# A one-layer streaming encoder on one core: the right-hand side of SBUF moved by 64 bytes, the first gate's row fetched behind the first convolution block, and the stored blocks of W_out split during z's first four tiles

## The chip, the core and the metric

The kernel runs on one NeuronCore of a Trainium2 chip. The core has five engines, each with its own instruction queue in program order: PE (TensorE, matrix products into PSUM), DVE (VectorE), ACT (ScalarE), POOL (GpSimd) and SP (SyncE, which here only issues DMAs). They wait for one another through semaphores. SBUF holds 128 partitions; a tile's address below is its byte offset in each partition. A matmul has a stationary operand, which is loaded into the array first (the rows PEld of the profile), and a moving one, which streams through it column by column; both come from SBUF. The metric is the device time of one execution in microseconds (us), the median of several runs.

## The reference

One layer for 1024 tokens of width 1024, all in float32. `c` gives six modulation vectors; `gate_m` scales the mixer's result and `gate_f` that of the feed-forward part.

```python
c_act = jax.nn.silu(c)
mod = (c_act @ w_ada[l] + b_ada[l])[:, None, :]
sh_m, sc_m, g_m, sh_f, sc_f, g_f = jnp.split(mod, 6, axis=-1)
h = rmsnorm(x, norm_mix_w[l]) * (1 + sc_m) + sh_m
z, xbc, dt_raw, q, k, v = jnp.split(h @ w_in[l], IN_SPLITS, axis=-1)
y_ssd = ssd_mixer(z, xbc, dt_raw, ssd_conv_w[l], ssd_conv_b[l], dt_bias[l], a_log[l],
                  d_skip[l], ssd_norm_w[l])
y_att = chunk_attention(q, k, v, rel_bias[l])
x = x + g_m * (jnp.concatenate([y_ssd, y_att], axis=-1) @ w_out[l])
h = rmsnorm(x, norm_ffn_w[l]) * (1 + sc_f) + sh_f
x = x + g_f * conv_ffn(h, w_up[l], ffn_conv_w[l], w_down[l])
return rmsnorm(x, final_norm_w)
```

`ssd_mixer` convolves `xbc` (eight blocks of 128 channels) causally over time, runs a state-space scan in chunks, and multiplies by `silu(z)`; `conv_ffn` is an up product, a short convolution, a gated silu and a down product.

## The kernel before

**Precision.** Every large product is made of three matmuls of fp32r operands: `mm3` (lines 84 to 86) multiplies high by high, high by low and low by high part. `split` (lines 88 to 94) makes the two parts: ACT copies the high one, DVE subtracts to get the low one; with a scale they are lines 90 and 91.

**Stages, in order of time.** The modulation and the first projections (0 to 97 us); attention with the other projections; the convolution blocks of `xbc` (`conv_silu`: 24 x 2 matmuls of 512 columns each, then the taps of line 651 on DVE and silu on ACT); z (`z_tile`: eight tiles for each of two column halves, 24 matmuls of 260 columns a tile); the scan with the product by W_out (`ssd_pre`, `ssd_y`, `wout_half`); the up stage (22 `Unit`s, each seven products of 12 matmuls of 512 columns into `uX`, `uY` and `uZ`); the down stage (seven products into `dn`). Up and down use a scheme of seven half-size products.

**Where operands lie.** SBUF is filled from both ends. The left pools hold constants, the ring homes `w0`, `w1` (pool `rw`) and `w2` (`wu`), the high and low parts of h (`hH`, `hL`, later `tH`, `tL`); the right ones hold `pad`, `ya`, the attention tiles, `xs`, z's weights `wzh` and `wzl`, and later `b11`, `b21`, `t1` and the ring homes `r12` and `r22` (`hq`). In the built program the left tiles lie 64 bytes past a multiple of 128 (w0 at 3520, w1 at 11712, w2 at 19904, hH0 at 36288), the right ones at a multiple (r12 at 106368, r22 at 114560, t1h at 122752, b11h at 163712, ya at 212864); matmuls start at such addresses plus multiples of 128. `pad` (line 180) is never read or written: its size sets where the right side starts.

**The ring.** Split weights of the up stage, and both split operands of the down stage, take their homes in turn, so that the home of each `w` is known from its place in the order:

```python
HOMES = ((rw, "w0"), (rw, "w1"), (wu, "w2"), (hq, "r12"), (hq, "r22"))
FIRST, AGAIN = (0, 1, 2, 0, 1, 3, 4), (2, 0, 1, 3, 4)
```

In the down stage each step splits first the moving operand, then the stationary one.

**The first gate and W_out.** `mod_col` loads a row block of `w_ada` and reduces it on DVE; `conv_mods` spreads these over the convolutions. The columns of `gate_m` are added up in `gcol` (line 911), turned into rows by a matmul and an ACT copy, written to DRAM (`cols_to_dram`, lines 149 to 152) and read back as a row for all partitions (line 924) into `rowb` and `gm1`. W_out comes in eight slots of 128 x 1024. `wout_load` fetches a slot in two DMAs, `wout_fold` (line 737) multiplies a slot of the first column half by the gate's row, `wout_store` splits slots 4 to 7 and writes high and low parts to DRAM, `wout_split` splits slots 0 to 3 into h's place once z no longer reads it, `wout_back` fetches the stored ones. Slots 0 and 1 are staged in `wst`, the others in three thirds of `wos`: 4 and 7 share the first, 5 and 2 the second, 6 and 3 the third, so the later load of each pair waits for the earlier slot's store. Slots 4 to 7 are split at tiles 3 to 6 of z's second half (column half 1, which is computed first).

**z's weights.** `wz_weights` loads a half in four pieces through the two halves of `raws`, so that pieces 3 and 4 load only when pieces 1 and 2 are split.

**What sets the order.** A scheduler with a timing model orders each engine's instructions at build time, so a step may stand elsewhere than its line suggests.

Of the kernel before, what the change touches and what calls it, by code (L numbers as in the profile page):

```python
# [72 lines left out]
def tile_block(ctx: ExitStack, tc: tile.TileContext, x, ccol, pk, w_ada, w_first, w_ft, w_z,  # L73
               w_out, w_up, w_down, bias, fnw, out, dbg=None):
    nc = tc.nc
    V, A, T = (InOrder(tc, e) for e in (nc.vector, nc.scalar, nc.tensor))
# [20 lines left out]
    const = ctx.enter_context(tc.tile_pool(name="const", bufs=1))  # L97
# [12 lines left out]
    modc = const.tile([P, 48], F32, name="modc")  # L110
# [28 lines left out]
    def raw_tile(n=1024):  # L139
        rawc[0] += 1  # L140
        return raws[:, rawc[0] % 2, 0:n]

    def mod_col(ft, t, at=None):
        nc.sync.dma_start(t, w_ada[ft])
        with tc.issue_after(at) if at else ExitStack():
            V.tensor_tensor_reduce(out=t, in0=t, in1=rowa, scale=1.0, scalar=0.0,
                                   op0=ALU.mult, op1=ALU.add, accum_out=modc[:, ft:ft + 1])

    def cols_to_dram(cols, ps, t, d):
        T.matmul(ps, cols, ident, start=True, stop=True)  # L150
        A.activation(t, ps, AF.Copy)
        nc.sync.dma_start(d, t)
# [3 lines left out]
    def wu_pair(src, hieng, loeng):  # L156
        t = raw_tile()
        nc.sync.dma_start(t, src)
        wh = wu.tile([P, 1024], F32R, tag="wh", name="wh")
        if not wls:  # L160
            wls.append(wu.tile([P, 2, 1024], F32R, tag="w2", bufs=1, name="wl"))
        wl = wls[0][:, rawc[0] % 2, :]
        split(wh, wl, t, hieng, loeng)
        return wh, wl
# [12 lines left out]
        return ap.rearrange("p (a b) -> p a b", a=4)  # L177

    pad = ctx.enter_context(tc.tile_pool(name="pad", bufs=1, side="right"))
    pad.tile([P, 24], F32, name="pad")  # L180
    es_y = ExitStack()
    yp = es_y.enter_context(tc.tile_pool(name="yp", bufs=1, side="right"))
    es_at = ExitStack()
# [82 lines left out]
    def s_tile():  # L266
        return ps1.tile([P, 1024], F32, tag="s", bufs=2, name="s")
# [93 lines left out]
    for j in range(2):  # L361
        k = slice(4 * j, 4 * j + 4)
# [43 lines left out]
    for hh in range(2):  # L406
# [13 lines left out]
        for kt in range(KT):  # L420
            if hh == 0:
# [7 lines left out]
                t = raw_tile(768)  # L429
# [73 lines left out]
    def tp_tile():  # L503
        return pst.tile([P, 512], F32, tag="tp", bufs=2, name="tp")
# [139 lines left out]
    def conv_silu(ft, dst):  # L644
        wh, wl = early.pop(ft) if ft in early else wu_pair(w_ft[ft], A, V)
        ps = s_tile()
        gemm_ft(wh, wl, [ps[:, 0:512], ps[:, 512:1024]])
        w = [pkt[:, SCW + 4 * ft + j:SCW + 4 * ft + j + 1] for j in range(4)]
        A.activation(dst, ps, AF.Identity, scale=w[3], bias=pkt[:, SCB + ft:SCB + ft + 1])
        for j in range(1, 4):  # L650
            last = V.scalar_tensor_tensor(dst[:, j:S], ps[:, 0:S - j], w[3 - j], dst[:, j:S],
                                          op0=ALU.mult, op1=ALU.add)
        for hh in range(2):
            c = slice(hh * 512, hh * 512 + 512)
            A.activation(dst[:, c], dst[:, c], AF.Silu)
        return last.ins
# [18 lines left out]
    def th512():  # L675
        return thp.tile([P, 512], F32, tag="th", bufs=2, name="th")
# [16 lines left out]
    gm1 = es_g.enter_context(tc.tile_pool(name="gmp", bufs=1, side="left")).tile([P, 512], F32, name="gm1")  # L693
# [5 lines left out]
    def conv_mods(n, at):  # L699
        for _ in range(CMODS[n]):  # L700
            k = wosc[0]
            wosc[0] += 1
            t = xs[:, 2 * (k % 4):2 * (k % 4) + 2, :].rearrange("p a b -> p (a b)") if n < 5 else wos[:, k % 3, :]
            mod_col(todo.pop(0), t, at)

    conv_mods(0, last_v[0])
    for g in range(2):
        conv_mods(2 * g + 1, conv_silu(4 + g, bt_[g]))
        conv_mods(2 * g + 2, conv_silu(6 + g, ct_[g]))
    G.memset(ones, 1.0)  # L710
    G.affine_select(out=tle, in_=ones, compare_op=ALU.is_ge, fill=0.0, base=0,
# [17 lines left out]
    def wout_load(slot):  # L729
        (dh, j), t = WORDER[slot], stage(slot)  # L730
        for b in range(2):
            nc.sync.dma_start(t[:, b * 512:(b + 1) * 512], w_out[order[2 * j + b], :, halves[dh]])
        return t

    def wout_fold(t):
        tv = t.rearrange("p (a b) -> p a b", a=2)
        V.tensor_tensor(tv, tv, rowb[:, 0:512].unsqueeze(1).to_broadcast([P, 2, 512]), ALU.mult)
# [14 lines left out]
    def wout_store(slot, t):  # L752
        h = bcp.tile([P, D], F32R, tag="rm", bufs=2, name="woh")
        for b in range(2):
            c = slice(512 * b, 512 * b + 512)
            k = SNW + order[2 * WORDER[slot][1] + b]
            split(h[:, c], t[:, c].bitcast(F32R), t[:, c], A, V, scale=pkt[:, k:k + 1])
        nc.sync.dma_start(wsd[slot - 4][0], f32(h))
        nc.sync.dma_start(wsd[slot - 4][1], t)
# [3 lines left out]
            nc.sync.dma_start(f32(t), d)  # L763

    wsd = [[dram.tile([P, D], F32, name=f"ws{n}{k}") for n in "hl"] for k in range(4)]
    gmd, gfd = (dram.tile([8, P], F32, name=n) for n in ("gmd", "gfd"))
    acd = dram.tile([64, P], F32, name="acd")

    def rows_from(d, k, n):
        return d[k:k + n].unsqueeze(0).to_broadcast([P, n, P])  # L770

    wzp = es_t.enter_context(tc.tile_pool(name="wzp", bufs=1, side="right", reuse_waits="tile"))

    def wz_weights(ch):
        ws = []
        for a in range(4):
            th_ = wzp.tile([P, 2, 288], F32R, tag="wzh", bufs=WZB, name="wzh")[:, :, 0:260]
            tl_ = wzp.tile([P, 2, 288], F32R, tag="wzl", bufs=WZB, name="wzl")[:, :, 0:260]
            t = raw_tile(520)
            nc.sync.dma_start(t, w_z[ch, :, a * 520:(a + 1) * 520])  # L780
            split(th_, tl_, t.rearrange("p (a b) -> p a b", a=2), A, V, scale=(0.5, None)[ch])
            ws.append((th_, tl_))
        return ws
# [83 lines left out]
    def ssd_pre(c, xp_, between=None):  # L867
# [38 lines left out]
        return xdt, xdd, cb, ms_  # L906

    wz = wz_weights(1)
    gcol = const.tile([P, 16], F32, name="gcol")
    gbias = [pkt[:, B_ADA + o:B_ADA + o + 8] for o in (G_M, G_F)]  # L910
    V.tensor_tensor(gcol[:, 0:8], modc[:, G_M:G_M + 8], gbias[0], ALU.add)
    WORDER = [(0, 0), (0, 1), (1, 0), (1, 1), (0, 2), (0, 3), (1, 2), (1, 3)]
    wt = {}

    def wout_get(*slots):
        for j in slots:
            wt[j] = wout_load(j)

    for st in range(NT):
        z_tile(1, st, wz)  # L920
        if st == 0:
            cols_to_dram(gcol[:, 0:8], tp_tile()[0:8, 0:P], th512()[0:8, 0:P], gmd)
            for t, k in ((rowb[:, 0:512], 0), (gm1, 4)):
                nc.sync.dma_start(t.rearrange("p (a b) -> p a b", a=4), rows_from(gmd, k, 4))
            wout_get(0, 1, 4, 5, 6)
        if st == 2:
            V.tensor_tensor(gcol[:, 8:16], modc[:, G_F:G_F + 8], gbias[1], ALU.add)
            cols_to_dram(gcol[:, 8:16], tp_tile()[0:8, 0:P], th512()[0:8, 0:P], gfd)
        if st in (3, 4, 5, 6):
            j = st + 1  # L930
            if j < 6:
                wout_fold(wt[j])
            wout_store(j, wt[j])
            if j == 4:
                wout_get(7)
        if st in (6, 7):
            wout_fold(wt[st - 6])
    wz = wz_weights(0)
    wout_get(2, 3)
    for st in range(NT):  # L940
# [170 lines left out]
    for c in range(NT):  # L1111
        if c == 1:
            ssd_turn(*turn)
        y, t = ssd_y(c, *pre)
# [10 lines left out]
        n, k = ((0, slice(0, 3)), (2, slice(0, 4)), (3, slice(0, 3)))[c] if c < 3 else (c + 1, slice(0, 3))  # L1125
# [622 lines left out]
```

## Time and profile before

| | us |
|---|---|
| median of 3 runs (1190.01 to 1191.69) | 1190.08 |
| the profiled execution | 1191.6 |
| its span | 1189.9 |
| PE busy | 1162.9 |
| DVE busy | 910.1 |
| ACT busy | 587.5 |
| POOL busy | 163.0 |
| convolutions | about 255 to 355 |
| z | 355.6 to 409 |
| scan and W_out | 409 to 540 |
| up stage | 540 to 968 |
| down stage | 968 to 1185 |

The span is what the profile covers; the execution's own time has 1.7 us around it. A row of the timeline gives start, duration, engine, line, operation, output and inputs (buffer numbers left out), shape and count; in brackets stands how long the engine had been idle before it and what it waited for. A matmul's duration is modelled and longer than the distance to the next one, since they are pipelined: the pace is read from the starts. For `dn<-w` both operands are tiles called `w`.

### The profile page before, as it was taken

To read this page: it belongs to the slowest core of one execution; us is meant where nothing else is said; L and a number is where in the kernel's file an instruction comes from. 1 tells how busy PE (TensorE), PEld (TensorE's weight loads), DVE (VectorE), ACT (ScalarE), POOL (GpSimd) and SP (SyncE) were. 2 spreads that over 40 slices of the span, in tenths; PEclk is the share of its full clock that TensorE was granted. 3 is DMA by queue.
4 is the path that set the end of the run, shared out by engine and by line. 5 is a ranking of instruction groups with operands and counts; after the bars stand their busy time and mean duration, and the time that the engine had idled before them with its cause. 6 is when DMAs were issued, how large, how long until landed. Compare 5 with 4: busy or idle time off the path is not lost.

```text
span 1189.9 us, 15790 instructions
## 1 busy us (share of the span) xinstructions
PE 1162.9 (98%) x5839; PEld 974.3 (82%) x5839; DVE 910.1 (76%) x1357; ACT 587.5 (49%) x971; POOL 163.0 (14%) x179
## 2 busy tenths in 40 slices
PE   8999999999999999999999999999999999999996
PEld 7778888788889888887788888888888888888885
DVE  7746565687775778559999988898888869666986
ACT  5636555664334666586443444334533444433454
POOL 1103343440000266200000000000000000000522
PEclk9999999999999999999999999999999999999999
DMA  9736334254455722241223322332233378633443
GB/s 350 259 85 163 94 119 117 56 178 134 141 202 203 297 98 80 72 141 36 98 107 133 116 79 92 113 131 79 83 106 115 116 277 298 238 122 119 158 135 148
DMA packets 63741, 169.15 MB, mean 142 GB/s; under 512 B 6880, under 2 KB 7344, under 8 KB 62256
## 3 DMA queue, kind: packets, MB, share of 16 engines
q1 hardware_dynamic: 56320, 143.11, 36.1%
q10 hardware_dynamic: 7344, 25.04, 5.4%
q8 instruction: 46, 0.75, 0.3%
q14 instruction: 31, 0.25, 0.1%
HBM read 125.87 MB, written 32.81 MB: 133 GB/s over the span
## 4 chain that ended last, share of the span: by engine, by line
PE 81%; DVE 11%; ACT 3%; issue 3%; DMA 1%; POOL 1%; POOLq 0%; DVEq 0%; ACTq 0%
PE wops L854 6%; PE dn L86 5%; PE dn L84 5%; PE dn L85 5%; PE uY L84 5%; PE uY L86 5%; PE uY L85 5%; PE uX L86 3%; PE uX L84 3%; PE uZ L85 3%; PE uZ L84 3%; PE uX L85 3%; PE uZ L86 3%; PE s L84 3%; PE s L86 3%
## 5 line engine op out<-in xcount | busy, mean ns | idle before, releaser
L85 PE MATMUL dn<-w 128*128 128x512 f32 x296 | 108.1, 391 | 0.0
L84 PE MATMUL dn<-w 128*128 128x512 f32 x296 | 108.1, 391 | 0.0
L86 PE MATMUL dn<-w 128*128 128x512 f32 x296 | 100.2, 391 | 0.2 <-DVE w L94 0.2
L84 PE MATMUL uY<-tH,w 128*128 128x512 f32 x248 | 97.2, 392 | 0.0
L85 PE MATMUL uY<-tL,w 128*128 128x512 f32 x248 | 97.0, 391 | 0.0
L86 PE MATMUL uY<-tH,w 128*128 128x512 f32 x248 | 96.9, 391 | 0.0
L1609 POOL TENSOR_TENSOR ya<-ya,xs 128x512 f32<-128x512 f32 x4 | 17.2, 4334 | 557.4 <-ACT xs L1605 557.4
L93 ACT ACTIVATE w<-ya 128x1024 fp32r<-128x1024 f32 (+1 forms) x41 | 39.2, 957 | 87.2 <-PE uY L86 84.2
L854 PE MATMUL wops<-hH,yhl 128*128 128x512 f32 x224 | 73.0, 398 | 1.0 <-DVE yhl L94 1.0
L86 PEld LDWEIGHTS dn<-w 128*128 128x128 f32 x296 | 55.4, 188 | 13.3 <-DVE w L94 1.1
L535 POOL TENSOR_SCALAR p<-p,st 128x640 f32<-128x640 f32 (+4 forms) x64 | 50.3, 794 | 115.9 <-DVE st L534 113.0
L84 PEld LDWEIGHTS dn<-w 128*128 128x128 f32 x296 | 55.5, 188 | 12.4
L85 PEld LDWEIGHTS dn<-w 128*128 128x128 f32 x296 | 55.5, 188 | 12.2
L93 ACT ACTIVATE w<-xs 128x1024 fp32r<-128x1024 f32 (+1 forms) x41 | 39.1, 954 | 38.6 <-PE uY L86 33.3
L529 DVE CUSTOM_DVE_ANT_0 p<-s,bias 128x640 f32<-128x640 f32 (+4 forms) x58 | 38.3, 674 | 23.1 <-PE tp L561 8.8
L86 PEld LDWEIGHTS uY<-tH,w 128*128 128x128 f32 x248 | 46.6, 188 | 10.5
L84 PEld LDWEIGHTS uY<-tH,w 128*128 128x128 f32 x248 | 46.6, 188 | 10.3
L85 PEld LDWEIGHTS uY<-tL,w 128*128 128x128 f32 x248 | 46.5, 188 | 10.2
L532 ACT ACTIVATE p<-p,st 128x640 f32<-128x640 f32 (+4 forms) x64 | 44.1, 692 | 18.0 <-DVE st L529 17.3
L94 DVE TENSOR_TENSOR pt<-tp,pt 128x512 fp32r<-128x512 f32 (+2 forms) x72 | 41.8, 595 | 13.1 <-ACT pt L93 12.8
L1283 DVE SCALAR_TENSOR_TENSOR a<-cv,pkt,a 128x1023 f32<-128x1023 f32 (+1 forms) x40 | 51.0, 1278 | 0.1
L84 PE MATMUL s<-hH,wh 128*128 128x512 f32 x128 | 50.5, 395 | 0.1
(503 smaller groups left out, 3402.0 us busy)
## 6 DMA issues: line engine op xcount, KB each, us to landing
gz<-a ACTq DMA_DIRECT2D x10, 1024.0 KB, 5.0
ya<-in_w_up_dram SPq DMA_DIRECT2D x11, 768.0 KB, 4.2
xs<-in_w_up_dram SPq DMA_DIRECT2D x11, 768.0 KB, 4.1
adat<-in_w_ada_dram SPq DMA_DIRECT2D x16, 512.0 KB, 5.8
xs<-in_w_ada_dram SPq DMA_DIRECT2D x16, 512.0 KB, 4.5
raws<-in_w_ft_dram SPq DMA_DIRECT2D x15, 512.0 KB, 3.9
qk<-qk SPq DMA_DIRECT2D x56, 128.0 KB, 2.3
gy<-a ACTq DMA_DIRECT2D x10, 512.0 KB, 2.6
```

Source lines behind the costliest of these rows:

```text
L84: T.matmul(ps, lh, rh, start=start, stop=False, skip_group_check=more)
L85: T.matmul(ps, lh, rl, start=False, stop=False, skip_group_check=more)
L86: T.matmul(ps, ll, rh, start=False, stop=stop, skip_group_check=more)
L93: i = A.activation(hi, src, AF.Copy) if ehi is A else ehi.tensor_copy(hi, src)
L94: return i, elo.tensor_tensor(lo, src, f32(hi), ALU.subtract)
L529: V.tensor_tensor_reduce(out=dst, in0=src, in1=bsl, scale=-1.0, scalar=3e38, op0=ALU.add, op1=ALU.min, accum_out=nm)
L532: A.activation(pv_, pv_, AF.Exp, scale=-1.0, bias=nm, accum_out=rs)
L535: last_g.append(G.tensor_scalar(pv_, pv_, rr, 1.0, op0=ALU.mult, op1=ALU.mult).ins)
L854: i = op(*a, **k)
L1283: V.scalar_tensor_tensor(a[:, j:S], c[:, 0:S - j], w[2 - j], a[:, j:S], op0=ALU.mult, op1=ALU.add)
L1609: G.tensor_tensor(src, src, fnr[:, halves[1]], ALU.mult)
```

## The change

- `pad` has 8 floats instead of 24, so every tile of the right side lies 64 bytes higher; the left side stays. All matmul operands then lie 64 bytes past a multiple of 128.
- The columns of `gate_m`, their way through DRAM and the two row loads stand after the first convolution block (`g == 0`) instead of before and in z's first tile.
- In z's first tile the W_out slots are asked for in the order 4, 5, 6, 0, 1 instead of 0, 1, 4, 5, 6.
- Slots 4 to 7 are folded (the first two) and stored at tiles 0 to 3 instead of 3 to 6, and slots 0 and 1 are folded at tiles 4 and 5 instead of 6 and 7.

```diff
-    pad.tile([P, 24], F32, name="pad")
+    pad.tile([P, 8], F32, name="pad")
...
+    gcol = const.tile([P, 16], F32, name="gcol")
+    gbias = [pkt[:, B_ADA + o:B_ADA + o + 8] for o in (G_M, G_F)]
     conv_mods(0, last_v[0])
     for g in range(2):
         conv_mods(2 * g + 1, conv_silu(4 + g, bt_[g]))
+        if g == 0:
+            V.tensor_tensor(gcol[:, 0:8], modc[:, G_M:G_M + 8], gbias[0], ALU.add)
+            cols_to_dram(gcol[:, 0:8], tp_tile()[0:8, 0:P], th512()[0:8, 0:P], gmd)
+            for t, k in ((rowb[:, 0:512], 0), (gm1, 4)):
+                nc.sync.dma_start(t.rearrange("p (a b) -> p a b", a=4), rows_from(gmd, k, 4))
         conv_mods(2 * g + 2, conv_silu(6 + g, ct_[g]))
...
     for st in range(NT):
         z_tile(1, st, wz)
         if st == 0:
-            cols_to_dram(gcol[:, 0:8], tp_tile()[0:8, 0:P], th512()[0:8, 0:P], gmd)
-            for t, k in ((rowb[:, 0:512], 0), (gm1, 4)):
-                nc.sync.dma_start(t.rearrange("p (a b) -> p a b", a=4), rows_from(gmd, k, 4))
-            wout_get(0, 1, 4, 5, 6)
+            wout_get(4, 5, 6, 0, 1)
...
-        if st in (3, 4, 5, 6):
-            j = st + 1
+        if st in (0, 1, 2, 3):
+            j = st + 4
             if j < 6:
                 wout_fold(wt[j])
             wout_store(j, wt[j])
             if j == 4:
                 wout_get(7)
-        if st in (6, 7):
-            wout_fold(wt[st - 6])
+        if st in (4, 5):
+            wout_fold(wt[st - 4])
```

Each engine has the same instructions as before, in another order at a few places. On DVE, from the second gate's columns (`gcol`) on, with the taps of the last convolution (`xst`), z's bias adds (`zs`) and the folds (`wos` or `wst` with `rows`), before:

```order
L927 TENSOR_TENSOR gcol_3530<-modc_71,pkt_66 128x8
L651 SCALAR_TENSOR_TENSOR xst_3424<-s_3429,pkt_66,xst_3424 128x1023
L651 SCALAR_TENSOR_TENSOR xst_3424<-s_3429,pkt_66,xst_3424 128x1022
L798 TENSOR_TENSOR zs_2912<-zps_3532,pkt_66 128x8
L651 SCALAR_TENSOR_TENSOR xst_3424<-s_3429,pkt_66,xst_3424 128x1021
L798 TENSOR_TENSOR zs_2912<-zps_3578,pkt_66 128x8
L798 TENSOR_TENSOR zs_2912<-s_3605,pkt_66 128x8
L798 TENSOR_TENSOR zs_2912<-s_3638,pkt_66 128x8
L737 TENSOR_TENSOR wos_2922<-wos_2922,rows_67 128x1024 x2
L737 TENSOR_TENSOR wst_3566<-wst_3566,rows_67 128x1024
L737 TENSOR_TENSOR wst_3569<-wst_3569,rows_67 128x1024
```

and after:

```order
L929 TENSOR_TENSOR gcol_2929<-modc_71,pkt_66 128x8
L749 TENSOR_TENSOR wos_2922<-wos_2922,rows_67 128x1024
L651 SCALAR_TENSOR_TENSOR xst_3435<-s_3440,pkt_66,xst_3435 128x1023
L651 SCALAR_TENSOR_TENSOR xst_3435<-s_3440,pkt_66,xst_3435 128x1022
L806 TENSOR_TENSOR zs_2912<-zps_3539,pkt_66 128x8
L749 TENSOR_TENSOR wos_2922<-wos_2922,rows_67 128x1024
L651 SCALAR_TENSOR_TENSOR xst_3435<-s_3440,pkt_66,xst_3435 128x1021
L749 TENSOR_TENSOR wst_3575<-wst_3575,rows_67 128x1024
L91 SCALAR_TENSOR_TENSOR wos_2922<-wos_2922,pkt_66,woh_3579 128x512 x2
L806 TENSOR_TENSOR zs_2912<-zps_3588,pkt_66 128x8
```

The four folds stood in a row behind the fourth bias add; now two stand between the last taps and one behind them (the fourth stands eight rows above the first of these), and the low splits of the stored slots (`wos` with `woh`) follow at once.

On ACT, from the first high split of z's second weights (`wzh_3807`) to the copy of the decay rows (`th_3876`), before:

```order
L90 ACTIVATE wzh_3807<-raws_68 128x2x260
L90 ACTIVATE wzh_3812<-raws_68 128x2x260
L797 ACTIVATE zs_2912<-s_3779 128x252
L809 ACT_TABLE_LOAD
L809 ACTIVATE sm_e_2913<-sm_p_2916 128x64
L90 ACTIVATE woh_3771<-wos_2922,pkt_66 128x512 x2
L90 ACTIVATE wzh_3817<-raws_68 128x2x260
L90 ACTIVATE wzh_3822<-raws_68 128x2x260
L801 ACTIVATE zs_2912<-zps_3831 128x260
L829 ACTIVATE th_3876<-tp_3879 128x128
L801 ACTIVATE zs_2912<-zps_3921 128x260
```

and after:

```order
L90 ACTIVATE wzh_3807<-raws_68 128x2x260
L90 ACTIVATE wzh_3812<-raws_68 128x2x260
L805 ACTIVATE zs_2912<-s_3780 128x252
L817 ACT_TABLE_LOAD
L817 ACTIVATE sm_e_2913<-sm_p_2916 128x64
L90 ACTIVATE wzh_3817<-raws_68 128x2x260
L90 ACTIVATE wzh_3822<-raws_68 128x2x260
L809 ACTIVATE zs_2912<-zps_3831 128x260
L809 ACTIVATE zs_2912<-zps_3921 128x260
L809 ACTIVATE zs_2912<-s_3948 128x260
L760 ACTIVATE hH0_84<-wst_3572 128x1024
L837 ACTIVATE th_3876<-tp_3879 128x128
```

The high split of the last stored slot (`woh`, two rows in one) is gone from between them, and `th_3876` has moved behind two more evictions of z (`zs`) and a split of slot 0 (`hH0` from `wst`).

On SP, from the high part of the third stored slot (slot 6) to the decay rows' store (`acd`), before:

```order
L758 DMA wsh2_3500<-woh_3737 128x1024
L732 DMA wos_2922<-in_w_out_dram 128x512 x2
L759 DMA wsl2_3501<-wos_2922 128x1024
L780 DMA raws_68<-in_w_z_dram 128x520 x2
L732 DMA wos_2922<-in_w_out_dram 128x512 x2
L758 DMA wsh3_3502<-woh_3771 128x1024
L732 DMA wos_2922<-in_w_out_dram 128x512
L759 DMA wsl3_3503<-wos_2922 128x1024
L732 DMA wos_2922<-in_w_out_dram 128x512
L830 DMA acd_3506<-th_3876 64x128
```

and after:

```order
L770 DMA wsh2_3511<-woh_3656 128x1024
L771 DMA wsl2_3512<-wos_2922 128x1024
L152 DMA gfd_2928<-th_3652 8x128
L770 DMA wsh3_3513<-woh_3690 128x1024
L744 DMA wos_2922<-in_w_out_dram 128x512
L771 DMA wsl3_3514<-wos_2922 128x1024
L744 DMA wos_2922<-in_w_out_dram 128x512 x3
L788 DMA raws_68<-in_w_z_dram 128x520 x2
L838 DMA acd_3515<-th_3876 64x128
```

The last two loads of z's weights (`raws`) stood between the loads of slots 2 and 3 (`wos` from `in_w_out`); now they stand behind all four of those and behind both parts of the last stored slot. The gate's row and its column, which stood some rows ahead of the first store, are no longer in this part: they stand behind a `w_ft` load among the `w_ada` loads of the convolutions.

More of the change, by code (lines that the diff above doesn't have):

```diff
@@ L704, in conv_mods, with rows_from @@
             mod_col(todo.pop(0), t, at)
+    gmd, gfd = (dram.tile([8, P], F32, name=n) for n in ("gmd", "gfd"))
+    def rows_from(d, k, n):
+        return d[k:k + n].unsqueeze(0).to_broadcast([P, n, P])
+    gcol = const.tile([P, 16], F32, name="gcol")
+    gbias = [pkt[:, B_ADA + o:B_ADA + o + 8] for o in (G_M, G_F)]
     conv_mods(0, last_v[0])
@@ L765, in tile_block @@
     wsd = [[dram.tile([P, D], F32, name=f"ws{n}{k}") for n in "hl"] for k in range(4)]
-    gmd, gfd = (dram.tile([8, P], F32, name=n) for n in ("gmd", "gfd"))
     acd = dram.tile([64, P], F32, name="acd")
-    def rows_from(d, k, n):
-        return d[k:k + n].unsqueeze(0).to_broadcast([P, n, P])
     wzp = es_t.enter_context(tc.tile_pool(name="wzp", bufs=1, side="right", reuse_waits="tile"))
@@ L908, in tile_block @@
     wz = wz_weights(1)
-    gcol = const.tile([P, 16], F32, name="gcol")
-    gbias = [pkt[:, B_ADA + o:B_ADA + o + 8] for o in (G_M, G_F)]
-    V.tensor_tensor(gcol[:, 0:8], modc[:, G_M:G_M + 8], gbias[0], ALU.add)
     WORDER = [(0, 0), (0, 1), (1, 0), (1, 1), (0, 2), (0, 3), (1, 2), (1, 3)]
```

## The prediction

> **What bounds the kernel now.** I read the page first, then busy times by stretch, then single matmuls by start time. The page:
>
> ```profile
> span 1189.9 us, 15790 instructions
> ...
> PE 1162.9 (98%) x5839; PEld 974.3 (82%) x5839; DVE 910.1 (76%) x1357; ACT 587.5 (49%) x971; POOL 163.0 (14%) x179
> ...
> PEclk9999999999999999999999999999999999999999
> ```
>
> TensorE (PE) covers 98% of the span at a full clock, so only two things can help: shorter steps from matmul to matmul, or fewer holes. The stretches show both cases (start and end, length, busy time of PE, its weight loads, DVE, ACT, POOL, then clock and DMA):
>
> ```profile
> 380.00:382.90 2.90, 1.98 (x15) 1.56 (x13) 2.90 (x8) 2.88 (x6) 0.00 (x0) 1.00 0.87 349
> ...
> 388.50:390.00 1.50, 0.48 (x5) 0.36 (x4) 1.36 (x7) 1.01 (x2) 0.00 (x0) 1.00 1.06 409
> ...
> 660.00:700.00 40.00, 40.00 (x176) 32.68 (x175) 35.56 (x44) 18.71 (x21) 0.00 (x0) 1.00 0.28 99
> 1060.00:1100.00 40.00, 40.00 (x177) 32.83 (x176) 29.94 (x38) 14.06 (x16) 0.00 (x0) 1.00 0.40 131
> ```
>
> In the up stage (660 to 700 us) and the down stage (1060 to 1100) PE never rests, and VectorE (DVE), the next engine, has 35.56 and 29.94 of 40 us: a matmul step shortened by some nanoseconds shortens the kernel. In the z stage there are two holes, at 380 to 382.9 and at 388.5 to 390.
>
> **First edit: the 64 bytes.** Busy rows can't show the matmul step, since each record's modelled 0.39 us overlaps the next. Starts can. Two stretches of 24 identical matmuls, `t1` moving against ring tiles:
>
> ```profile
> 670.20 0.39 PE L84 MATMUL uZ<-t1h,w 128*128 128x512 f32 x1
> ...
> 675.57 0.39 PE L86 MATMUL uZ<-t1h,w 128*128 128x512 f32 x1
> ...
> 708.78 0.39 PE L84 MATMUL uZ<-t1h,w 128*128 128x512 f32 x1
> ...
> 714.01 0.39 PE L86 MATMUL uZ<-t1h,w 128*128 128x512 f32 x1
> ```
>
> The first takes (675.57 - 670.20)/23 = 233.5 ns a step, the second (714.01 - 708.78)/23 = 227.4. Line, shape, moving tile and clock are the same; what differs is the ring home of the stationary `w`: homes w0 and w1 on the left (address 64 past a multiple of 128) in the first, r12 and r22 on the right (0 past) in the second. `t1` is on the right (0). The down stage has the ring's five homes in fixed pairs:
>
> ```profile
> 1099.64 0.39 PE L84 MATMUL dn<-w 128*128 128x512 f32 x1
> ...
> 1105.13 0.39 PE L84 MATMUL dn<-w 128*128 128x512 f32 x1
> ...
> 1110.73 0.39 PE L84 MATMUL dn<-w 128*128 128x512 f32 x1
> ...
> 1116.19 0.39 PE L84 MATMUL dn<-w 128*128 128x512 f32 x1
> ```
>
> Each interval is 24 steps: moving w1 (64), stationary r12 (0): 5.49/24 = 228.8 ns; moving r22 (0), stationary w2 (64): 5.60/24 = 233.3; moving w0, stationary w1 (both 64): 5.46/24 = 227.5. So a 512-wide step costs some 6 ns more when the moving operand is at 0 and the next stationary one at 64, about 1 ns more the other way round, and least when the residues agree. After the change every matmul operand lies at 64.
>
> Counted over the program, by moving operand and the next stationary one of equal width: 694 steps of 512 columns are at (0, 64): 188 down, 338 uX, 168 uZ. At 233.4 - 227.5, less 0.3 for the scatter among equal pairs, each gives 5.6 ns: **3.9 us**. Some 800 are at (64, 0): 635 in the up and down stages at 1 ns are **0.6 us**, and 168 in the first projection 0.1 more.
>
> The sign turns for narrower matmuls:
>
> ```profile
> 91.97 0.34 PE L66 MATMUL vps<-wsh,hH 128*128 128x256 f32 x1
> ...
> 97.38 0.28 PE L66 MATMUL vps<-wsh,hL 128*128 128x256 f32 x1
> ...
> 279.64 0.28 PE L572 MATMUL pv<-pt,v 128*128 128x256 f32 x1
> ...
> 280.47 0.28 PE L573 MATMUL pv<-pt,v 128*128 128x256 f32 x1
> ...
> 357.17 0.28 PE L84 MATMUL zps<-wzh,hH 128*128 128x260 f32 x1
> ...
> 362.05 0.28 PE L86 MATMUL zps<-wzh,hL 128*128 128x260 f32 x1
> ```
>
> `vps`, 256 columns at (0, 64), steps by 5.41/47 = 115.1 ns; `pv`, the same width at (0, 0), by 0.83/7 = 118.6. So about 100 `vps` in PE's dense part lose 3.5 ns each: -0.4 us. The 384 z matmuls (260 columns, (0, 64)) step by 4.88/41 = 119.0; `pv`'s step with four columns more would be about 120.7: -0.65 us, kept for the z stage. That price is bounded by 0 and by the 3.5 ns of `vps` (-1.3 us). Some 420 transposes go from (64, 0) to (64, 64); no row has such a pair at both residues. Their bounds are -3.5 ns (a loss, as `vps`) and +5.9 (a gain, as uZ), half of them where PE is dense: -0.7 to +1.2 us; I take 0, between the nearest in width and the 1 ns of their own direction. DVE and ScalarE (ACT) are costed at nothing: tiles of both sides already take the same time there (the `wos` and `wst` folds of line 737 each have 1.22 us).
>
> Sum of the move: 3.9 + 0.6 + 0.1 - 0.4 = **4.2 us**, with 0.65 to come off below. Equal pairs can never save more than 6.1 × 694 and 1.5 × 800 ns, 5.4 us.
>
> The Trainium skill says otherwise: in "SBUF — State Buffer", section Who interferes with whom, PE's moving operand and its weight load have independent read ports, and "PE and ACT never wait on anyone". By that, where the right side lies is worth 0 instead of 4.2 us. The 233.5 against 227.4 contradicts it for two streams of PE itself, unless it is the side that matters; that is rival A.
>
> **Second edit: the gate's row and the stores.** What is late in the z stage, by the engines' own rows:
>
> ```profile
> 299.95 0.33 SPq L158 DMA_DIRECT2D raws<-in_w_ft_dram  x1
> ...
> 352.39 3.09 SPq L732 DMA_DIRECT2D wos<-in_w_out_dram  x6
> ...
> 369.96 0.35 SPq L924 DMA_DIRECT2D rows<-gmd  x1
> ...
> 384.38 1.54 SPq L780 DMA_DIRECT2D raws<-in_w_z_dram  x2
> ```
>
> ```profile
> 370.39 0.17 DVE L798 TENSOR_TENSOR zs<-s,pkt 128x8 f32<-128x8 f32 x1 [3.70 <-ACT zs L797]
> 373.50 2.36 DVE L737 TENSOR_TENSOR wos<-wos,rows 128x1024 f32<-128x1024 f32 x2 [2.94 <-DMA rows<-gmd]
> ...
> 382.25 1.30 DVE L91 SCALAR_TENSOR_TENSOR wzl<-raws,wzh 128x520 fp32r<-128x520 f32 x2
> ```
>
> ```profile
> 380.81 1.15 ACT L90 ACTIVATE wzh<-raws 128x520 fp32r<-128x520 f32 x2
> ...
> 388.95 1.31 ACT L90 ACTIVATE wzh<-raws 128x520 fp32r<-128x520 f32 x2 [1.16 <-DMA raws<-in_w_z_dram]
> ...
> 394.60 0.28 ACT L829 ACTIVATE th<-tp 128x128 f32<-128x128 f32 x1
> ...
> 400.74 2.45 ACT L883 ACTIVATE cr<-cr,acc 128x128 f32<-128x128 f32 x8 [1.10 <-DMA cr<-acd]
> ```
>
> ```profile
> 381.82 0.28 PE L84 MATMUL s<-wzh,hH 128*128 128x260 f32 x1
> 382.99 0.39 PE L85 MATMUL zps<-wzl,hH 128*128 128x260 f32 x1 [0.89 <-DVE wzl L91]
> ...
> 388.34 0.28 PE L86 MATMUL s<-wzh,hL 128*128 128x260 f32 x1
> 389.64 0.51 PE L84 MATMUL zps<-wzh,hH 128*128 128x260 f32 x2 [1.02 <-ACT wzh L90]
> ...
> 409.26 0.55 PE L854 MATMUL ydp<-xdt,th 128*128 128x64 f32 x3
> ```
>
> The gate's row lands at 373.4; only then do the folds start (1.2 us each, four), the splits behind them on DVE, and behind those z's second weights: `wzl` at 382.25, and after it frees `raws`, the last loads at 384.38, whose data PE awaits until 389.64. By starts, a 0.119 us step took 1.17 and 1.30 us: holes of 1.05 and 1.18. With two smaller ones (0.3 at 381, 0.4 at 396.6) 2.9 us are there to win.
>
> After, the row is fetched at about 301 us, behind a `w_ft` load. It costs SyncE (SP) 0.35 + 1.24 (its column's landing) + 0.35 + 0.42 = 2.4 us; the `w_ada` loads queued behind feed DVE only. The columns' matmul and copy move from 368 to 300 (about 0.2 us of PE, both places dense: 0). The folds stand among conv taps and z's bias adds, where DVE idles (2.94 and 3.70 us above); the first awaits its `w_out` half, about 357 (issued by 352.8, with the 4.5 us median below), so the last conv's taps run some 2 us late, silu ends near 365, and its transposes, which now stand near 366, don't wait.
>
> ```profile
> wos<-in_w_out_dram SPq DMA_DIRECT2D x12, 256.0 KB, 4.5
> ...
> wsl<-wos SPq DMA_DIRECT2D x4, 512.0 KB, 3.5
> raws<-in_w_z_dram SPq DMA_DIRECT2D x5, 260.0 KB, 4.6
> ```
>
> Slot 4's low half then goes out about 366, lands at 369.5; slot 7 loads until 374, is split by 376.5, stored at 377. `wzh` waits then only for PE's release of the old weights near 378.7, and `wzl` is done by 380.7, about when PE wants it. The last w_z loads now stand behind all four loads of slots 2 and 3 (gone by 379), leave as `wzl` frees `raws` and land near 385; they are split by 386.5, as PE, with 5.6 us of work on the first halves (382.9 to 388.5 before), asks for them. Then the chain to the scan: ACT copies `th` behind a 1.05 us `hH` copy now, at about 392 instead of 394.6; `cr` lands about 398 instead of 400.7; the first masked product is ready near 403.8, and PE gets there near 407 (409.26 less what is won). So 2.9 won, less 0.65 for z's step, less 0.25 for a rest of the two tight places: **2.0 us**, between 0 and 2.9.
>
> **Sum:** 4.2 + 2.0 = 6.2 us. The profiled execution is 1191.6 us (span 1189.9 and 1.7 around it): 1185.4. The median is 1.5 below it, so I predict 1190.1 - 6.2 = **1183.9 us**.
>
> **Rivals.**
> A, the side and not the address: a pair on one side might be fast because it is on one side, and the move then does nothing. Every fast pair above is also a pair of one side; against it, one sort of mixed pair costs 6 ns and the other 1, as if phases met. Then z alone, 2.0 + 0.65: 1187.4.
> B, z gives nothing: the early weights end in another wait, first of all `th` behind `hH` on ACT (1.05 us more than before) and `cr`'s landing, with a margin of 3 us by estimates from medians. Then 4.2 - 0.65: 1186.5.
> C, slower: slot 7's load lands late. On ACT its two copies stand ahead of three z evictions and `wzh`, so every us past about 376 is one on PE. It decides at 382, where 6 us are lost; at 385 PE starts on z's second weights near 388.7, loses 8.2 where it lost 2.5, and with 3.5 from the move the time is 1192.3. Against it: issued at 369.5, the load would need 12 us to reach 382, where the median is 4.5.
> D, both A and B: 1190.
>
> **How the numbers follow.** Forecast 0.64, A 0.10, B 0.16, C 0.04, D 0.06. The forecast's own range, from the bounds (move 2.5 to 6.6 with the transposes, z 0.7 to 2.9), is 1181 to 1187. The range reaches A and B: 1181.0 to 1187.6. Within 0.2%, 2.4 us, a measurement of this kernel can't be told from no change: faster than 1187.7 is the forecast, B and most of A (0.88), same is D and the rest (0.08), slower 0.04.
>
> **What would show it.** Right: steps of 227 to 228 ns in every uX, uZ and `dn` stretch, none at 233; z steps near 120.7; no hole over 0.5 us at 380 to 390; `rows<-gmd` near 301. Wrong: steps of 233 that remain (A), a wait at the scan's first `ydp` (B), or ACT waiting for slot 7's load ahead of `wzh` (C).

## The result and the profile after

| | before | after |
|---|---|---|
| median, us | 1190.08 (1190.01 to 1191.69) | 1180.99 (1179.54 to 1182.93) |
| ratio | | 0.9919, 95% interval 0.9904 to 0.9934 |
| profiled execution | 1191.6 | 1180.9 |
| its span | 1189.9 | 1179.2 |
| granted TensorE clock | 0.997 | 0.997 |

The kernel became 9.1 us faster by the medians and 10.7 us by the profiled executions. 6.2 us were predicted: direction and places were right, the size was too small, and the measured median lies at the very edge of the predicted range, just outside it. The two differences disagree by 1.6 us because the profiled execution of before was the slowest of its four (1191.6 against a median of 1190.08); in the later comparisons the median of before was 1190.85, 1191.97, 1192.3 and 1191.7, and beside the last the changed kernel had 1180.27, so 10 or 11 us is nearer than 9.

The page of the changed kernel (busy time of each engine, its share of the span):

```profile
span 1179.2 us, 15793 instructions
...
PE 1154.7 (98%) x5839; PEld 974.9 (83%) x5839; DVE 907.4 (77%) x1357; ACT 587.9 (50%) x971; POOL 162.2 (14%) x179
```

The same number of PE instructions, PE still at 98%: nothing was removed, the steps and holes shrank. Next the four stretches whose rows of before stand in the prediction, in the changed kernel (start and end, length, busy time of PE, its weight loads, DVE, ACT, POOL, then clock and DMA):

```profile
380.00:382.90 2.90, 2.90 (x27) 2.90 (x26) 1.65 (x4) 1.96 (x4) 0.00 (x0) 1.00 1.00 391
388.50:390.00 1.50, 1.50 (x15) 1.50 (x14) 1.33 (x7) 0.00 (x0) 0.00 (x0) 1.00 0.04 11
660.00:700.00 40.00, 40.00 (x178) 33.14 (x177) 36.04 (x43) 17.36 (x20) 0.00 (x0) 1.00 0.33 114
1060.00:1100.00 40.00, 40.00 (x178) 33.10 (x178) 30.24 (x38) 16.89 (x22) 6.23 (x1) 1.00 0.37 117
```

The holes at 380 to 390 us are gone (2.90 of 2.90 and 1.50 of 1.50 us, where it was 1.98 and 0.48), and 40 us of the up stage now hold 178 matmuls instead of 176. The clock stands at 1.00 in both, so a faster clock isn't the cause. The starts that the prediction compared, at the same places of the program:

```profile
665.41 0.39 PE L84 MATMUL uZ<-t1h,w 128*128 128x512 f32 x1
...
670.62 0.39 PE L86 MATMUL uZ<-t1h,w 128*128 128x512 f32 x1
...
703.49 0.39 PE L84 MATMUL uZ<-t1h,w 128*128 128x512 f32 x1
...
708.71 0.39 PE L86 MATMUL uZ<-t1h,w 128*128 128x512 f32 x1
...
1089.73 0.39 PE L84 MATMUL dn<-w 128*128 128x512 f32 x1
...
1095.17 0.39 PE L84 MATMUL dn<-w 128*128 128x512 f32 x1
...
1100.61 0.39 PE L84 MATMUL dn<-w 128*128 128x512 f32 x1
...
1106.05 0.39 PE L84 MATMUL dn<-w 128*128 128x512 f32 x1
```

The first `t1` stretch takes 5.21/23 = 226.5 ns a step (233.5 before), the second 5.22/23 = 227.0 (227.4). The three intervals of `dn` are 5.44 us each, 226.7 ns a step, where they were 228.8, 233.3 and 227.5. Every kind of pair became quicker, the one that the prediction took for the best too.

### The profile page after: what moved, and what is told of

It reads as the page before. It is cut to its first block, busy times and chain, and to the rows that moved or that the text cites. A ratio compares the mean times of both kernels' runs of the same rounds, so it can differ in the third digit from the quotient of the medians.

```text
span 1179.2 us, 15793 instructions
## 1 busy us (share of the span) xinstructions
PE 1154.7 (98%) x5839; PEld 974.9 (83%) x5839; DVE 907.4 (77%) x1357; ACT 587.9 (50%) x971; POOL 162.2 (14%) x179
## 4 chain that ended last, share of the span: by engine, by line
PE 82%; DVE 11%; ACT 3%; issue 3%; POOL 1%; POOLq 0%; DVEq 0%; ACTq 0%
PE wops L862 5%; PE dn L86 5%; PE dn L84 5%; PE dn L85 5%; PE uY L86 5%; PE uY L84 5%; PE uY L85 5%; PE uX L86 3%; PE uZ L84 3%; PE uZ L85 3%; PE uZ L86 3%; PE uX L84 3%; PE uX L85 3%; PE s L84 3%; PE s L86 3%
```

## Experiments

Where the time went is read by stage, from the first matmul of a stage to the first of the next (the down stage to its last `dn`), in each kernel's profile (in us; "step" is the mean start-to-start of the 512-wide matmuls in the up and down stages, without the few over 300 ns). "R" and "L" are where the right-hand and left-hand operands of the up and down stages lie, modulo 256 bytes.

| kernel | R, L | z | scan, W_out | up | down | step, ns | median | ratio to before, interval |
|---|---|---|---|---|---|---|---|---|
| before | 128, 192 | 53.70 | 131.11 | 427.38 | 212.26 | 229.6 | 1190.08 | 1 |
| changed | 192, 192 | 49.83 | 130.67 | 422.05 | 210.11 | 226.8 | 1180.99 | 0.9919 (0.9904 to 0.9934) |
| move_alone | 192, 192 | 54.03 | 131.27 | 422.25 | 209.81 | 226.8 | 1183.64 | 0.9936 (0.9923 to 0.9948) |
| gate_alone | 128, 192 | 49.39 | 130.81 | 427.17 | 212.20 | 229.6 | 1186.0 | 0.9961 (0.9948 to 0.9975) |
| both_at_0 | 128, 0 | 49.90 | 130.69 | 428.03 | 212.65 | 230.1 | 1188.22 | 0.9978 (0.9969 to 0.9987) |
| equal_at_0 | 0, 0 | 50.35 | 130.69 | 422.05 | 209.80 | 226.8 | 1179.97 | 0.9901 (0.9887 to 0.9916) |
| apart_256 | 192, 192 | 49.74 | 130.67 | 422.05 | 210.01 | 226.8 | 1180.45 | 0.9907 (0.9893 to 0.9921) |
| no_pad | 224, 192 | 51.17 | 130.66 | 429.00 | 213.01 | 230.8 | 1190.71 | 0.9992 (0.9982 to 1.0001) |
| right_at_32 | 160, 192 | 49.78 | 130.70 | 428.79 | 212.68 | 230.6 | 1189.44 | 0.9986 (0.9977 to 0.9995) |
| t1_off | 192, 192; ring's right homes 64, t1 128 | 49.74 | 130.67 | 427.68 | 212.40 | 229.9 | 1188.5 | 0.9974 (0.9963 to 0.9985) |
| t1_only | 192, 192; t1 128 | 49.74 | 130.73 | 423.86 | 210.19 | 227.5 | 1182.38 | 0.9921 (0.9907 to 0.9934) |
| row_only | 192, 192 | 51.78 | 131.43 | 422.04 | 209.80 | 226.8 | 1181.41 | 0.9919 (0.9905 to 0.9932) |
| stores_only | 192, 192 | 53.84 | 131.23 | 422.30 | 210.14 | 226.8 | 1185.02 | 0.9944 (0.9931 to 0.9956) |
| row_only_again | 192, 192 | 51.43 | 131.59 | 422.04 | 209.77 | 226.8 | 1182.93 | 0.9930 (0.9917 to 0.9942) |
| changed_again | 192, 192 | 49.74 | 130.71 | 422.09 | 210.34 | 226.8 | 1180.27 | 0.9904 (0.9889 to 0.9919) |
| wz_off | 192, 192; z's weights 128 | 49.86 | 130.67 | 422.03 | 209.97 | 226.9 | 1179.97 | 0.9902 (0.9889 to 0.9916) |

### The two edits apart: move_alone, gate_alone

move_alone, on the kernel before:

```diff
-    pad.tile([P, 24], F32, name="pad")
+    pad.tile([P, 8], F32, name="pad")
```

> The kernel before with the right-hand side moved by 64 bytes and nothing else. Theory (phases: a matmul step is quick when its two operands have the same address modulo 128): every 512-wide step in uX, uY, uZ and dn near 227 ns, as in the changed kernel's trace, where these stages are 7.4 us shorter (4.3 from the 694 steps at (0, 64), 1.8 from the 635 at (64, 0), 1.4 from equal pairs); less 0.4 for vps and 0.3 for z's steps: 6.7 us below before, 1183.4. The holes of the z stage stay. By the prediction's own terms (4.2 less 0.65) it would be 3.6 below, 1186.5. Rival (the 7.4 us come partly from the z stage's new timing, since DMA and VectorE meet PE at other moments): steps near 227 only in part, 4 to 5 us below.

gate_alone is the changed kernel with that line put back to 24.

> The changed kernel with the right-hand side back at its old address. Theory: the z stage's holes of 1.05 and 1.19 us and its small ones are gone, worth 3.2 us, z's steps stay at 119 ns, the up and down stages keep 233 ns at (0, 64): 1186.9. By the prediction's term (2.9 less 0.25) 2.65 below: 1187.4. Rival (the holes close only because the move changes z's steps): a hole above 0.5 us at 380 to 390 remains and the time is 1188.5 or more.

Both held. The move alone gives the whole of the up and down stages: 427.38 to 422.25 and 212.26 to 209.81, 7.6 us, against 4.5 us in the prediction; it costs 0.33 us in z (53.70 to 54.03). Its up and down stages (same columns as above):

```profile
541.20:963.45 422.25, 420.63 (x1858) 347.47 (x1856) 375.37 (x455) 189.46 (x216) 0.93 (x1) 1.00 0.32 112
963.45:1173.26 209.81, 209.75 (x924) 173.10 (x923) 166.82 (x190) 94.19 (x125) 30.33 (x14) 1.00 0.51 176
```

The gate's edit alone leaves those stages within 0.3 us of before and gives 4.3 us in z. The z stage of gate_alone and the two stages behind it:

```profile
354.19:403.58 49.39, 49.39 (x417) 49.03 (x416) 32.98 (x68) 29.15 (x63) 0.56 (x1) 1.00 0.70 257
534.39:961.55 427.16, 426.01 (x1857) 347.39 (x1856) 375.64 (x455) 189.77 (x216) 0.93 (x1) 1.00 0.31 111
961.55:1173.75 212.20, 212.18 (x924) 172.94 (x923) 169.37 (x190) 94.19 (x125) 27.91 (x14) 1.00 0.52 174
```

PE is busy for all of z's 49.39 us: no hole is left to close. The ratios multiply to 0.9936 x 0.9961 = 0.990, and the changed kernel had 0.9919 and, run again, 0.9904. By stages the two edits add up: 0.33 less 4.31 makes -3.98 us in z, where the changed kernel has -3.87.

### What about the address counts: both_at_0, equal_at_0, apart_256

both_at_0 puts the right-hand side back and moves the left-hand one by 64 bytes, so that both are at 0 modulo 128. Against the changed kernel:

```diff
-    pad.tile([P, 8], F32, name="pad")
+    pad.tile([P, 24], F32, name="pad")
...
     gcol = const.tile([P, 16], F32, name="gcol")
+    const.tile([P, 16], F32, name="lpad")
```

> The changed kernel with the right-hand side back at 0 past a multiple of 128 and the left-hand side moved by 64 bytes to 0 as well. Theory (phases: only equality counts): steps of 227 ns everywhere in the up and down stages, within 1 us of the changed kernel: 1180 to 1182. Rival (64 past a multiple of 128 is itself the good place): the steps stay at the 227.9 ns that (0, 0) pairs had before or above, 2.5 us or more over the changed kernel. Rival (the right side must move): as gate_alone, near 1187.

The theory as the prediction had it, residues modulo 128, fell here. All operands agree modulo 128, and the kernel is slower than gate_alone, where they don't. Its up and down stages:

```profile
537.83:965.86 428.03, 427.08 (x1857) 347.91 (x1856) 375.83 (x455) 190.03 (x216) 0.93 (x1) 1.00 0.31 111
965.86:1178.51 212.65, 212.64 (x925) 173.28 (x923) 169.28 (x190) 94.09 (x125) 27.93 (x14) 1.00 0.51 172
```

428.03 us instead of 422.05. Modulo 256 the sides are 128 apart in this kernel, 64 apart before, and equal after the change; with that, a new theory was at hand. equal_at_0 has a pad of 56 floats beside the `lpad` (both sides at 0 modulo 256); apart_256 has a pad of 72 floats and no `lpad` (equal modulo 256, 256 apart modulo 512).

> The changed kernel with both sides at 0 past a multiple of 256 (in the changed kernel both are at 192; in the run with both sides at 0 modulo 128 the left was at 0 and the right at 128 modulo 256). Theory (equality modulo 256): every 512-wide step in uX, uY, uZ and dn near 226.7 ns on average, 1180 to 1182. Rival (192 modulo 256 is itself the good place, or the left side must not move): means of 228 and more, 1186 or more.

> The changed kernel with the right-hand side 256 bytes lower: left and right agree modulo 256, and 256 apart modulo 512. Theory (modulo 256): as the changed kernel, 226.7 ns, 1180 to 1182. Rival (the modulus is 512 or more): mixed pairs at 229 to 233 ns, 1186 to 1189.

Both came out by the new theory, at 1179.97 and 1180.45 us. The stages of equal_at_0:

```profile
536.06:958.11 422.05, 420.61 (x1858) 347.47 (x1856) 375.28 (x455) 189.45 (x216) 0.93 (x1) 1.00 0.32 112
958.11:1167.91 209.80, 209.72 (x925) 173.10 (x923) 166.69 (x190) 94.19 (x125) 30.32 (x14) 1.00 0.51 176
```

So neither the place 192 nor the move itself matters: what counts in these two stages is that both operands of a matmul start at the same address modulo 256.

### How near is near enough: no_pad, right_at_32

no_pad leaves the pad tile out; right_at_32 makes it 16 floats. The sides are 32 bytes apart, in one 64-byte block or in two.

> The changed kernel without the pad tile: right at 224, left at 192 modulo 256, 32 bytes apart but in one 64-byte block. Theory (the addresses must be equal): mixed pairs above 226.7 on average, 228 to 233 by the direction, equal pairs lifted by the hang-over: 1184 to 1189. Rival (it is the 64-byte block that counts): steps at 226.7 throughout, 1180 to 1182.

> The changed kernel with the right-hand side 32 bytes lower: right at 160, left at 192 modulo 256, 32 bytes apart and in two different 64-byte blocks. Theory (the addresses must be equal): as without the pad tile, with the directions exchanged: 1184 to 1189. Rival (the 64-byte block counts): like 64 bytes apart, 233 and 229 ns, 1186 to 1187.

Both are slow, no_pad as slow as the kernel before in spite of the better z stage (1190.71; z 51.17), so it isn't the block of 64 bytes. Both lie above the 1184 to 1189 us expected, because both directions turned out dear at 32 bytes. (Kernels with the whole of the gate's edit had z stages of 49.4 to 51.2 us; what sets that was not followed.) Sorted by each matmul's moving address minus its stationary address, modulo 256, the mean step over all 512-wide matmuls of the up and down stages is:

| apart | 0 | +32 | +64 | 128 | -64 | -32 |
|---|---|---|---|---|---|---|
| step, ns | 226.8 | 233.2 to 233.3 | 229.5 | 232.7 | 233.2 | 233.2 |
| from | changed, equal_at_0, apart_256, move_alone | no_pad, right_at_32 | before, gate_alone | both_at_0 | before, gate_alone | no_pad, right_at_32 |

In every kernel with mixed pairs, its equal pairs were slower too: 227.9 ns in before, gate_alone and both_at_0, 228.5 in no_pad, 228.2 in right_at_32, against 226.8 where all are equal. t1_off, below, fits in, with 227.6 for its equal pairs, 232.8 at 128 and 233.2 at -64; its 96 steps at +64 took 230.7.

The first projection shows a limit of this. Its 512-wide steps that follow one another (147 of them) were at +64 before and are equal after the change, and took 230.2 and 230.1 ns. They stand in short runs between narrower matmuls; only from the ninth step of a run on (37 steps) do they differ, 229.0 before and 226.9 after. Against +64, equal addresses pay in long runs alone, which fits what follows.

### Why equal pairs were slow beside mixed ones: t1_off, t1_only

t1_off was meant to put `t1` alone out of step; as its pad also moved the ring's right-hand homes below it by 128 bytes, it was in fact a second case of 128 apart.

```diff
+    hca.tile([P, 16], F32, tag="o1", name="o1")
     h_new(hca, "t1")
+    hca.tile([P, 16], F32, tag="o2", name="o2")
```

> The changed kernel with t1 alone at 0 past a multiple of 128, everything else at 64. The 168 uZ steps with t1 moving are then (0, 64). Theory: they take 233 to 234 ns again (+1.1 us), and the uY steps with equal pairs that follow each of them begin at 230 to 237 ns and need some steps to come back to 227 (a hang-over, +0.1 to 0.4 us); uX and dn stay at 227: 1182.2 to 1182.6. Rival (equal pairs were slow before for another reason, such as VectorE and ScalarE working across the two sides): uY stays at a mean of 227.0 throughout, +1.1 us alone.

Neither theory had 1188.5 us. It was the miss that, with both_at_0, led to the modulus of 256: `dn`, which never reads `t1`, went from 210.11 to 212.40 us, as its ring tiles were now at 192 and 64. t1_only makes the first of the two pads 48 floats, so that the homes below move by 256 bytes.

> The changed kernel with t1 alone 64 bytes lower (128 modulo 256) and, unlike the run t1_off, with the ring's right-hand homes still at 192 modulo 256 as everything else. Theory (equality modulo 256): only uZ's steps with t1 moving, 264 of them, take 233 ns again (+1.7 us); the uY or uX steps that follow each stretch of them begin at 228 to 236 ns and come back to 226.7 within about five steps (+0.02 us a time, 0.3 to 0.5 in all); dn stays at 226.7 on average, unlike the 229.7 of t1_off: 1182.7 to 1183.3. Rival (t1's place itself, or a phase lost once, slows everything behind it): uX, uY and dn at 229 and more, 1187 to 1189.

```profile
536.75:960.61 423.86, 422.40 (x1858) 347.31 (x1856) 375.23 (x455) 189.46 (x216) 0.93 (x1) 1.00 0.32 112
960.61:1170.79 210.18, 209.98 (x924) 172.99 (x923) 166.59 (x190) 94.19 (x125) 30.30 (x14) 1.00 0.52 175
```

The up stage is 1.8 us longer, the down stage untouched. The 264 steps with `t1` average 233.3 ns, 6.5 over the rest, 1.7 us. Around the first of them:

```profile
549.58 0.39 PE L66 MATMUL uZ<-t1h,w 128*128 128x512 f32 x1
...
555.18 0.39 PE L66 MATMUL uY<-tH,w 128*128 128x512 f32 x1
```

24 steps in 5.60 us, 233.3 ns each. The `uY` steps behind them, equal pairs, are by the trace's starts 226, 235, 229, 232, 231, 227, 226, 227, 227 ns, and then 226 or 227 for good: a hang-over of about 20 ns that dies out in five steps. A like sequence (230, 236, 229, 232, 231, 227) follows a plain wait of PE at 579 us in the changed kernel. So PE's steps have a settled rhythm of 226, 227, 227 ns, and what breaks it costs some steps until it is back. All of it was some 0.2 us in t1_only (0.3 to 0.5 had been expected), as there are only 12 stretches of `t1`; in before, with mixed and equal pairs in turn all through, the equal ones lost 1.1 ns over 1463 steps, 1.6 us. That loss is the hang-over: by the operands' addresses in the built program and the trace's starts, the 626 equal steps at most eight behind an unequal pair (or behind one whose moving operand and next stationary one differ) average 229.3 ns and hold nearly all of the 1.6 us; the 772 further in average 226.9.

### Which half of the second edit: row_only, stores_only, row_only_again, changed_again

row_only is the changed kernel with the second half of the edit undone (`wout_get(0, 1, 4, 5, 6)`, folds and stores at tiles 3 to 6), stores_only with the first half undone (the gate's row fetched at z's first tile).

> The changed kernel with the gate's row fetched early, but the stored blocks' folds, splits and loads written where they were before (tiles 3 to 6). Theory (the lateness of the row alone made the holes; once it is there early the scheduler puts the folds early by itself): no hole above 0.5 us at 380 to 396, the z stage within 0.5 us of the changed kernel's, 1180 to 1182. Rival (the place of the stores does the work): the holes at 382 and 388 stay, 2 to 3 us over the changed kernel, 1183 to 1184.

> The changed kernel with the stored blocks' folds, splits and loads written early, but the gate's row fetched late, as before. Theory (the row is what is late): holes of 1 us and more at 382 and 388 as before, 2.5 to 3.2 us over the changed kernel, 1183.4 to 1184.2. Rival (the place of the stores does the work): the holes are gone or halved, 1181 to 1182.5.

stores_only held in its mechanism, though its median of 1185.02 lies 0.8 us above the range: its z stage is that of move_alone, 53.84 against 54.03. Its rows of SyncE's queue, of VectorE, and of PE with a wait:

```profile
368.52 0.35 SPq L925 DMA_DIRECT2D rows<-gmd  x1
```

```profile
372.01 2.36 DVE L744 TENSOR_TENSOR wos<-wos,rows 128x1024 f32<-128x1024 f32 x2 [2.89 <-DMA gm<-gmd]
```

```profile
381.50 0.39 PE L85 MATMUL zps<-wzl,hH 128*128 128x260 f32 x1 [0.88 <-DVE wzl L91]
...
388.32 0.51 PE L84 MATMUL zps<-wzh,hH 128*128 128x260 f32 x2 [1.16 <-ACT wzh L90]
```

With the row late the scheduler can't use the earlier place: the folds wait for the row as before, and the same two holes follow. (Its median is 1.4 us over move_alone's; the stages of the two profiles show no such difference from z on.) row_only is less plain. Its median was 0.4 us over the changed kernel's, yet its profile has a z stage of 51.78 us, 2 us longer. Both were run again.

> The kernel of row_only once more. Its median there was 0.4 us over the changed kernel's, but its profiled execution, the slowest of its four, had a z stage of 51.8 us against 49.8, with waits of 0.4 us at 387.6 and 395.1 and 0.8 us ahead of the scan. Theory (the row alone closes the holes, and that execution had a late load): a z stage of 49.7 to 50.3 us. Rival (the early stores are worth some 2 us by themselves): 51.5 us or more again, and 1.5 to 2.5 us over the changed kernel in the median.

> The changed kernel once more, for the scatter between executions. The stretch from the first vps step to the first projection of the features (17 to 131 us) took 113.3 us before, 113.8 after and 111.9 to 114.4 in the other profiles, without relation to their edits. Theory (this stretch scatters from one execution to the next, the rest does not): z stage 49.8, up stage 422.0, down stage 209.8 to 210.1 within 0.3 us again, the first stretch anywhere between 111.8 and 114.5. Rival (the differences belong to the edits): 113.8 again within 0.3 us.

changed_again measured 1180.27 us, with stages of 49.74, 130.71, 422.09 and 210.34. row_only_again measured 1182.93, with 51.43 in z and 131.59 in the scan: 2.6 us over in the two, and 2.7 in the median. The rival held. The rows of PE with a wait in the first row_only:

```profile
388.05 0.52 PE L84 MATMUL zps<-wzh,hH 128*128 128x260 f32 x2 [0.23 <-ACT wzh L90]
...
395.55 0.39 PE L66 MATMUL s<-wzh,hH 128*128 128x260 f32 x1 [0.23 <-DVE zs L810]
...
408.40 0.77 PE L862 MATMUL ydp<-xdt,th 128*128 128x64 f32 x5 [0.62 <-DVE zs L810]
```

The early row closes the hole at 382 and most of that at 388 (z from 54.0 to 51.4 to 51.8 us); the last w_z loads still leave later than in the changed kernel (382.25 us in row_only_again, 381.44 there), and what is left of the lateness reaches the scan. The early stores take the remaining 1.6 to 2 us in z and 0.8 in the scan, and are worth nothing without the row. As to changed_again's own question: the stretch from the first `vps` to 131 us was 113.74 us again (113.75 before it), so the 111.9 to 114.4 us in the other profiles are not plain scatter. What sets them stays open; it was not tried. Against the 113.3 us of before they move a kernel's total by up to 1.5 us, which is why the argument goes by stages.

### A narrower matmul: wz_off

```diff
     wz = wz_weights(1)
+    wzp.tile([P, 16], F32, tag="zpad", name="zpad")
```

> The changed kernel with z's weights alone 64 bytes lower, where they were before: z's 260-wide steps have mixed pairs, everything else equal ones. Theory (for steps of 260 columns the mixed pair is the quicker one): z's steps from 119.9 back to 119.0 ns on average, 0.3 us less, 1180.3 to 1181; nothing else moves. Rival (z's step follows the same rule as the 512-wide ones): 120.5 ns and more, 0.2 us or more over the changed kernel.

The pad is allotted behind z's first weights, so that their pool grows by 64 bytes and its tiles move down. z's steps went from 119.9 to 118.9 ns, 0.4 us over 384 of them, but the stage didn't shorten (49.86 against 49.83): PE waits 0.4 us at 365.6 instead. The median is 1 us below the changed kernel's and 0.3 below changed_again's, and the intervals overlap. The two rows of a weight tile of z start 1152 bytes apart, so z's pairs never all agree modulo 256: by their addresses in the built program they lie at -64 and +64 in turn in before and wz_off (118.7 to 118.9 and 119.1 to 119.2 ns), at 0 and 128 in turn in the changed kernel (119.6 and 120.2). So the narrow matmuls have another order than the 512-wide ones, as the prediction said, and here it is worth too little to show in the median.

## Why the prediction came out as it did

The terms, against the profiled executions (10.7 us between them):

| term | predicted | measured | where |
|---|---|---|---|
| 512-wide steps, moving 64 below | 3.9 | 4.3 | 694 steps, the same matmuls before and after |
| 512-wide steps, moving 64 above | 0.6 | 1.8 | 635 steps |
| equal pairs | 0 | 1.3 | the rest of the two stages, 7.5 us together |
| first projection | 0.1 | -0.1 | sum of its steps |
| `vps` | -0.4 | -0.5 | its step, 116.1 to 119.2 ns where two follow one another |
| z's step | -0.65 | -0.3 | z of before and of move_alone |
| z's holes | 2.65 | 3.8 | z of before and of gate_alone, less the moved column |
| transposes | 0 | 0.0 | sum of the `tp` steps |
| scan | 0 | 0.4 | 131.11 to 130.67 (130.81 in gate_alone, 131.27 in move_alone) |

**Right.** That a step is dearer where the two operands' addresses disagree, that the late row makes z's holes, and the places of both; that the two edits add; the sign and about the size for `vps`; that transposes don't care, and DVE and ACT hardly (910.1 to 907.4 and 587.5 to 587.9 us busy); that rivals A (the side), B (another wait in z's place), C (slot 7 late) and D don't occur. Slot 7 was split by 377.0 us and no wait stood ahead of the scan. The gate's row, fetched at 304.3 us instead of the 301 forecast, cost nothing that shows: its column's matmul lengthened the convolutions by 0.5 us (100.2 to 100.7), and z lost as much.

**The step that failed: the price of a 512-wide step against 227.5 ns.** The prediction took the pace of the best pair in the old trace, 227.5, for the pace of an equal pair, and so gave 1 ns to the pairs whose moving operand lies above and nothing to equal pairs, and capped the saving at 5.4 us. The runs show 226.8 for an undisturbed stream. Measured from there the pairs above cost 2.7 ns, those below 6.4, and equal ones, by the hang-over of their neighbours, 1.1. That is 3.0 us of the missing 4.5, and the 5.4 us that the prediction set as the most that equal pairs could save came to 7.5 in the two stages. The old trace had the evidence: equal pairs there averaged 227.9, with a median of 227, so their mean carried a tail that a stretch of 24 steps hides.

**Holes of the z stage were mis-sized.** The four holes that were summed, 2.9 us, left out two of 0.16 us (390.1 and 409.0 in the old trace) and the restart behind each wait, where one step takes 0.1 us more than its pace (five of them). With these it is 3.8, as measured, and the 0.25 us kept for a rest didn't occur. The price of z's step was too high: `pv`'s pace for four columns more makes 120.4 ns, not 120.7, and the trace has 119.9.

**The range.** The prediction's own bounds, 6.6 us for the move and 2.9 for z, make 1180.6 us, not the 1181 that it wrote; the measured median lies between the two. That would not have made the price of the step right: 1.2 of the 6.6 us stood for transposes, which gave nothing.

**The modulus was right by luck.** The prediction reasoned modulo 128. before and the changed kernel can't tell 128 from 256, since 64 bytes apart is unequal in both, but the advice would have been wrong: by it, both_at_0 should have been as fast as the changed kernel, and it is 7 us slower.

The Trainium skill's sentence from "SBUF — State Buffer", section Who interferes with whom, that "PE and ACT never wait on anyone", was weighed in the prediction. No run here was made to see whether another engine's reads slow PE; but equal_at_0 and both_at_0, which differ in where the right side lies alone, show that the distance between PE's own two operands costs 8 us of a kernel. That the two reads get in each other's way would be one reading of this; no run shows what happens inside PE.

## What to carry to other kernels

Where a stage is a solid stream of wide matmuls, read the step from the starts, sort it by the two operands' addresses, and compare with the quickest stream anywhere, not with the best pair of a mixed one: here, operands that agree modulo 256 bytes gave 226.8 ns, the other distances tried 229.5 to 233.3, and mixing costs the equal pairs too. A pad of a few floats per pool sets it, and any later edit of a pool's size can undo it, so it belongs among the things to measure again. When a late input holds up a chain, the input and the place of its consumers count together: moved alone, the consumers gained nothing and the input about half of the time in z and the scan.

## What was not expected of the hardware

In long runs of 512-wide fp32r matmuls the step depends on the two operands' distance modulo 256 bytes per partition; 32 bytes are enough, and the cost is uneven: +64 is the mildest (229.5 ns, 230.7 in t1_off), 32 either way as bad as -64 (233.2 to 233.3). And PE's pace has a memory of a few steps: after a wait or a mixed pair it comes back to 226, 227, 227 ns by way of steps such as 235, 229, 232, 231.
